# Modulation vectors of a two-block transformer: from split matmuls on TensorE to multiply-and-sum on VectorE

## The chip, the cores and the metric

One core of a Trainium2 chip runs the whole program. The metric is the time of one execution on the device in microseconds (us). The kernel before took 1823.71 us as the median of 3 runs (1823.54 to 1828.19). The profile is of one further execution, which took 1829.04 us; its span, from the first to the last instruction, is 1827.3 us. About 0.3% is what can be told from no change.

## The reference, cut to what matters

Two blocks of two layers each work on 256 tokens of width 1024. The second block also has 256 context tokens, and each of its layers is modulated by six vectors of width 1024 for the latent tokens and six for the context, made from two condition vectors `c` and `c_ctx`:

```python
def modulate(x, g, shift, scale):
    return rms_norm_2(x, g) * (1 + scale) + shift

for l in range(DEPTH):                       # 2
    need_ctx = l < DEPTH - 1
    mod_l = jnp.split((jax.nn.silu(c) @ ada_w[l] + ada_b[l])[:, None, :], 6, axis=-1)
    mod_c = jnp.split((jax.nn.silu(c_ctx) @ ada_w[l] + ada_b[l])[None, None, :], 6, axis=-1)
    hl = modulate(x_lat, norm_g[l, 0], mod_l[0], mod_l[1])
    hc = modulate(x_ctx, norm_g[l, 0], mod_c[0], mod_c[1])
    ...                                      # mixer (even_mixer, odd_mixer)
    x_lat = x_lat + mod_l[2] * (mix_l @ w_out[l])
    x_lat = x_lat + mod_l[5] * conv_ffn(modulate(x_lat, norm_g[l, 1], mod_l[3], mod_l[4]), ...)
    if need_ctx:
        ...                                  # the same for x_ctx with mod_c
```

`ada_w` is 2 x 1024 x 6144 in float32, so each layer's two products are a matrix of 1024 x 6144 times two vectors. In layer 1 the context gets only its first two vectors (shift and scale of the mixer's norm), because `need_ctx` is false there. Everything is in float32.

## The kernel before

All weights are read once, in the order of use, as units of up to 128 x 1056 float32 from one packed tensor `in_wts`. `fetch` (L471) takes the next unit: SyncE's queue starts the DMA into a slot of the ring `raw` (3 slots), ScalarE writes the rounded high half `wh` (L486), VectorE subtracts it and writes the low half `wl` (L487); these rings have 4 slots each. Every product then is three matmuls of fp32r: high by high, high by low, low by high (`tout` L506, `p_nout` L521). A low or high tile's slot comes free when the last matmul on it is done; so TensorE's progress lets ScalarE go on, and ScalarE lets VectorE go on.

The program is a list of steps (`plan` L1798), each with the units that it needs; before a step is emitted, units are fetched up to 5 ahead of it. `weave` puts two lists of steps together, evenly. The framework's scheduler then orders instructions on each engine; each engine works in that order and waits for semaphores.

The stages, with the stretch of the span that they take in the profile (read from the first and last instructions of each stage's lines, rounded): the first mixer of block 1 (0 to 200 us), FFN 0 (200 to 375), the second mixer (375 to 548), FFN 1 with the context attention of block 2 woven in (548 to 750), the even layer's mixer (750 to 1050), the third FFN, "f2" in the code (1050 to 1440), the odd layer's mixer (1440 to 1640), and the last FFN (1640 to 1827). The FFNs of block 1 work on 256 columns, the third FFN mostly on 512 (latent and context), the last on 258.

The modulation vectors are made in 24 blocks a layer, `p_ada` (L561): a block is 256 columns of `ada_w`, in two units. `csil` holds, for each 128 rows of the contraction, the two condition vectors after SiLU, split in high and low, and is the stationary operand; 16 matmuls of 256 columns accumulate four useful rows (L574 and L575). ScalarE copies them out (`adarow`, L578); two transposing products with `sel4` sum the halves and bring the result into columns (L581); VectorE adds the bias into `mods` (L583). `ADA` gives for each place of the plan how many blocks are woven in there; `ada_need(l, n)` brings the count up to what the next step needs.

Names in the rows: `acc` and `s` are PSUM tiles, `nh` and `nl` the split activations, `g`, `gh` and `gl` the gated FFN activations, `cc`, `gr`, `ur`, `ug` and `uu` FFN tiles, `o<-vx,W` and `s<-mqh,mkh` the even layer's recurrence in its parallel form.

Of the kernel before, what the change touches and what calls it, by code (L numbers as in the profile page):

```python
# [9 lines left out]
F32 = mybir.dt.float32  # L10
# [28 lines left out]
RAW_BUFS = 3  # L39
# [15 lines left out]
def unit_specs():  # L55
# [23 lines left out]
    for l in range(2):  # L79
        for i in range(24):  # L80
            halves(("ada", l, i), "ada_w_2", l, _ar(256 * i, 256))
# [94 lines left out]
def consts_all(i):  # L176
# [6 lines left out]
    cv = np.zeros((128, KD, 2), np.float32)  # L183
    cv[:, :, 0] = _tl(i["c_2"][0])
    cv[:, :, 1] = _tl(i["c_ctx_2"])
    c["cvec"] = cv.reshape(128, -1)
    s = np.zeros((128, 2))
    s[:4] = [[1, 0], [1, 0], [0, 1], [0, 1]]
    c["sel4"] = s
# [117 lines left out]
def weave(a, b, tail=0):  # L307
# [25 lines left out]
CN = 0  # L333
# [45 lines left out]
class Prog:  # L379
# [13 lines left out]
    def emit(self, tc, nc, ctx, wts, xin, cs, rpb, out, offs, probe=None):  # L393
        self.tc, self.nc, self.ctx = tc, nc, ctx
        self.wts, self.xin, self.cs, self.rpb, self.out, self.offs = wts, xin, cs, rpb, out, offs
        self.probe = probe or (lambda name, ap: None)
# [9 lines left out]

    def load_consts(self, pool, i):
# [4 lines left out]
    def start(self):  # L412
        nc = self.nc
        self.const = self.pool("const", 1)
        self.wp = self.pool("wp", 4)
        self.keep = self.pool("keep", 1)
# [29 lines left out]
        self.csil = self.keep.tile([128, 160], F32R, name="csil")  # L446
# [4 lines left out]
    def conditions(self):  # L451
        nc = self.nc
        sil = self.nat.tile([128, KD, 2], F32, name="sil")
        nc.scalar.activation(sil.rearrange("p a b -> p (a b)"), self.C["cvec"], AF.Silu)
        z = self.nat.tile([128, 128], F32, name="zz")
        nc.gpsimd.memset(z, 0.0)
        nc.scalar.activation(self.csil[:, 32:], z, AF.Copy)
        d = self.csil[:, :32].rearrange("p (k s e) -> p k s e", s=2, e=2)
        nc.scalar.activation(d[:, :, :, 0], sil, AF.Copy)
        nc.vector.tensor_sub(d[:, :, :, 1], sil, d[:, :, :, 0].bitcast(F32))  # L460
# [10 lines left out]
    def fetch(self, upto):  # L471
        nc = self.nc
        while self.next < min(upto, len(self.order)):
# [6 lines left out]
            nc.sync.dma_start(raw, src)  # L480
            h = self.wp.tile([128, nk, ncol], F32R, tag="wh", name="wh", bufs=HI_BUFS)
# [79 lines left out]
    def p_ada(self, l, i):  # L561
        steps = []
        box = Box()
        for kh in range(2):
            def f(i=i, kh=kh, box=box):
                nc = self.nc
                if kh == 0:
                    box.ps = self.acc()
                ps = box.ps
# [1290 lines left out]
```

## Time and profile before

| what | value |
|---|---|
| median of 3 runs | 1823.71 us |
| the profiled execution | 1829.04 us |
| its span | 1827.3 us |
| TensorE matmuls, weight loads busy | 1776.2 us (97%), 1686.5 us (92%) |
| VectorE busy | 1329.6 us (73%) |
| ScalarE busy | 1036.8 us (57%) |
| GpSimd busy | 66.1 us (4%) |
| TensorE clock granted, mean | 0.989 of full |
| weights and the rest from memory | 273.79 MB, 150 GB/s over the span |

Matmuls overlap: an instruction's duration in the trace is longer than the time from its start to the next one's start, and the time that it takes from TensorE is the latter. On VectorE a following instruction can start about 0.08 us before the end of the one ahead. "Idle before" and "waited for" name what ended an idle time; idle time on an engine that isn't the bound costs nothing by itself.

### The profile page before, as it was taken

The page shows a single profiled execution, that of the slowest core. Times are in us where ns is not written, and L with a number is a line of the kernel's source. Part 1 is how long each engine was busy: PE and PEld are TensorE (multiplying, and loading weights), DVE is VectorE, ACT ScalarE, POOL GpSimd, SP SyncE. Part 2 cuts the span into 40 slices and gives each one's busy share as a digit, 9 for nine tenths or more (in the row PEclk, how much of TensorE's full clock was granted, in tenths as well). Part 3 has the DMA queues.
Part 4 walks back from the last instruction along what each step waited for, and adds up shares of the span by engine and source line. Part 5 has one row for each costly group of instructions (what it writes and reads, how often), then busy time and mean ns, then how long its engine had stood idle before and what let it go on. Part 6 is the DMA issues. An engine that isn't in the chain of part 4 may idle for free.

```text
span 1827.3 us, 33701 instructions
## 1 busy us (share of the span) xinstructions
PE 1776.2 (97%) x13156; PEld 1686.5 (92%) x13156; DVE 1329.6 (73%) x2681; ACT 1036.8 (57%) x1807; POOL 66.1 (4%) x80
## 2 busy tenths in 40 slices
PE   8999999999999999999999999999999899999999
PEld 8998999999999999988988998888889899999999
DVE  6776887788878777866687796365467874669887
ACT  6776654566758667645445574243345565656554
POOL 0000000000110000000000000000000410000000
PEclk9999999999999999999999999999999999999999
DMA  7577555555554655535241463323335551245664
GB/s 242 165 224 223 175 185 175 183 184 181 154 170 156 186 169 166 177 113 173 84 137 47 139 186 127 103 93 108 101 96 153 165 161 49 85 139 171 195 188 138
DMA packets 80528, 277.03 MB, mean 152 GB/s; under 512 B 8945, under 2 KB 12145, under 8 KB 80241
## 3 DMA queue, kind: packets, MB, share of 16 engines
q1 hardware_dynamic: 79072, 272.25, 48.0%
q10 hardware_dynamic: 1296, 2.62, 0.4%
q8 instruction: 104, 1.70, 0.4%
q14 instruction: 56, 0.45, 0.1%
HBM read 273.79 MB, written 1.05 MB: 150 GB/s over the span
## 4 chain that ended last, share of the span: by engine, by line
PE 88%; DVE 6%; DMA 3%; ACT 2%; issue 1%; POOL 0%; ACTq 0%; DVEq 0%; POOLq 0%
PE acc L491 60%; PE s L491 20%; PE o L491 4%; DMA raw<-in_wts 3%; DVE wl L487 2%; ACT wh L486 2%; PE ptp L782 1%; PE tt L703 1%; PE stv L491 1%; DVE nt L1105 0%; PE ptp L772 0%; DVE nl L1108 0%; PE tt L798 0%; DVE t L734 0%; DVE x L818 0%
## 5 line engine op out<-in xcount | busy, mean ns | idle before, releaser
L486 ACT ACTIVATE wh<-raw 128x1024 fp32r<-128x1024 f32 (+2 forms) x528 | 540.6, 1031 | 474.4 <-PE acc L491 260.9
L487 DVE TENSOR_TENSOR wl<-raw,wh 128x1024 fp32r<-128x1024 f32 (+2 forms) x528 | 625.6, 1189 | 227.6 <-ACT wh L486 223.6
L491 PE MATMUL acc<-nh,wh 128*128 128x256 f32 (+2 forms) x872 | 271.5, 312 | 7.5 <-ACT wh L486 2.5
L491 PE MATMUL acc<-nh,wl 128*128 128x256 f32 (+2 forms) x872 | 270.5, 310 | 1.0 <-DVE wl L487 1.0
L491 PE MATMUL acc<-nl,wh 128*128 128x256 f32 (+2 forms) x872 | 270.2, 310 | 0.0
L491 PE MATMUL acc<-wh,nh 128*128 128x256 f32 (+2 forms) x768 | 222.5, 291 | 10.1 <-ACT nh L604 8.0
L491 PE MATMUL s<-nh,wh 128*128 128x256 f32 (+2 forms) x744 | 225.3, 303 | 0.9 <-ACT wh L486 0.9
L491 PE MATMUL s<-nh,wl 128*128 128x256 f32 (+2 forms) x744 | 225.0, 302 | 0.0
L491 PE MATMUL s<-nl,wh 128*128 128x256 f32 (+2 forms) x744 | 224.9, 302 | 0.0
L491 PE MATMUL acc<-wh,nl 128*128 128x256 f32 (+2 forms) x768 | 222.1, 291 | 0.5 <-DVE nl L1108 0.4
L491 PE MATMUL acc<-wl,nh 128*128 128x256 f32 (+2 forms) x768 | 221.3, 289 | 0.2 <-DVE wl L487 0.2
L491 PE MATMUL acc<-g,wh 128*128 128x256 f32 x1056 | 192.2, 283 | 0.5 <-DVE g L602 0.2
L491 PEld LDWEIGHTS acc<-nh,wh 128*128 128x128 f32 x872 | 166.2, 191 | 17.3 <-ACT wh L486 3.0
L491 PEld LDWEIGHTS acc<-nh,wl 128*128 128x128 f32 x872 | 166.2, 191 | 9.8 <-DVE wl L487 1.4
L491 PEld LDWEIGHTS acc<-nl,wh 128*128 128x128 f32 x872 | 166.2, 191 | 8.2
L491 PEld LDWEIGHTS acc<-g,wh 128*128 128x128 f32 x1056 | 163.2, 190 | 1.5 <-DVE x L818 0.9
L491 PEld LDWEIGHTS acc<-wh,nh 128*128 128x128 f32 x768 | 149.1, 194 | 11.3 <-ACT nh L604 8.3
L491 PEld LDWEIGHTS acc<-wh,nl 128*128 128x128 f32 x768 | 148.5, 194 | 2.3 <-DVE nl L1108 1.0
L491 PEld LDWEIGHTS acc<-wl,nh 128*128 128x128 f32 x768 | 149.0, 194 | 1.3 <-DVE wl L487 0.7
L491 PE MATMUL acc<-g,wl 128*128 128x256 f32 x528 | 147.5, 283 | 0.0
L491 PEld LDWEIGHTS s<-nh,wh 128*128 128x128 f32 x744 | 140.7, 189 | 7.1 <-ACT wh L486 1.1
L491 PEld LDWEIGHTS s<-nl,wh 128*128 128x128 f32 x744 | 140.8, 189 | 5.8
(378 smaller groups left out, 3548.3 us busy)
## 6 DMA issues: line engine op xcount, KB each, us to landing
raw<-in_wts SPq DMA_DIRECT2D x424, 512.0 KB, 4.0
raw<-in_wts SPq DMA_DIRECT2D x72, 448.0 KB, 3.3
raw<-in_wts SPq DMA_DIRECT2D x24, 384.0 KB, 3.6
x<-in_x SPq DMA_DIRECT2D x8, 256.0 KB, 6.9
raw<-in_wts SPq DMA_DIRECT2D x4, 408.0 KB, 3.0
rpb<-in_rpb ACTq DMA_DIRECT2D x1, 1536.0 KB, 8.3
raw<-in_wts SPq DMA_DIRECT2D x2, 528.0 KB, 4.0
out<-x ACTq DMA_DIRECT2D x8, 128.0 KB, 1.7
```

The lines of the kernel that those rows point to most:

```text
L486: nc.scalar.activation(hf[:, c], raw[:, c], AF.Copy)
L487: nc.vector.tensor_sub(lf[:, c], raw[:, c], hf[:, c].bitcast(F32))
L491: self.nc.tensor.matmul(o, a, b, start=start, stop=stop)
L703: self.nc.tensor.transpose(ps[:, p, t * 128:(t + 1) * 128], src[:, t, p * 128:(p + 1) * 128], self.ident)
L782: self.nc.tensor.transpose(pt[:, kb], P[:, kb * 128:(kb + 1) * 128], self.ident)
```

## The change

The host packs `ada_w` transposed, in 48 units a layer of 128 output columns by 1024 rows of the contraction, so that an output column is a partition and the sum runs along it. These units aren't split: the raw tile is used as it comes. `csil` becomes both condition vectors, broadcast to all partitions by one DMA (128 x 2048) and put through SiLU on ScalarE. For each unit VectorE multiplies the raw tile by a condition vector and sums along the partition, with the bias as start value, once for each condition, and only once (the latent condition) in layer 1 from unit 16 on. The product itself goes to a tile `junk` that nobody reads. The matmuls, the transposing products, `adarow`, `sel4` and the bias addition go.

The table `ADA` is new: 1 + 2 + 2 + 3 blocks (a block is now two units) in the first mixer, 5 in FFN 0, 7 in FFN 1, 4 in the even layer, 24 in the third FFN, none in the odd layer. In FFN 0, FFN 1 and the third FFN the units are woven over the whole stage. The raw ring has 4 slots. A pad of 64 bytes ahead of the weight pool and another behind it put the rings `raw`, `wh` and `wl` 64 bytes off a multiple of 128, and all else where it was by that measure. A DMA scratch area is made smaller, which gives the space.

```diff
-RAW_BUFS = 3
+RAW_BUFS = 4
...
-        for i in range(24):
-            halves(("ada", l, i), "ada_w_2", l, _ar(256 * i, 256))
+        for i in range(48):
+            add(("ada", l, i), "ada_w_2", l, _ar(128 * i, 128), rall)
...
+        if key[0] == "ada":
+            a = a.T
...
 ADA = {
...
-    "a1.0": 1, "o.m": 1, "a0.t": 0, "a0.1": 4, "f1": 1, "f2.0": 1, "f0": 0, "f2.1": 1, "e.3": 0, "a1.1": 2,
+    "a0.0": 1, "a0.1": 2, "a0.2": 2, "a0.3": 3, "f0": 5, "f1": 7, "e.0": 2, "e.1": 1, "e.2": 1, "f2": 24,
 }
...
+    def pad(self, name):
+        t = self.ctx.enter_context(self.tc.tile_pool(name=name, bufs=1)).tile([128, 16], F32, name=name)
+        self.nc.gpsimd.memset(t, 0.0)
...
+        self.pad("pad0")
         self.wp = self.pool("wp", 4)
+        self.pad("pad1")
...
+        c = self.csil.rearrange("p a b -> p (a b)")
+        nc.sync.dma_start(c, bass.AP(tensor=self.cond.tensor, offset=self.cond.offset, ap=[[0, 128], [1, 2 * D]]))
+        nc.scalar.activation(c, c, AF.Silu)
+        nc.gpsimd.memset(self.mods[1], 0.0)
...
             nc.sync.dma_start(raw, src)
+            if key[0] == "ada":
+                self.W[key] = raw
+                continue
...
-                h, w = self.W[("ada", l, i, kh)]
-                for k in range(4):
-                    c = 4 * (4 * kh + k)
-                    cs = self.csil[:, c:c + 128]
-                    self.mm(ps[:, :256], cs, h[:, k], kh == 0 and k == 0, False)
-                    self.mm(ps[:, :256], cs, w[:, k], False, kh == 1 and k == 3)
-                if kh == 1:
-                    row = self.small.tile([128, 256], F32, tag="adarow", name="adarow", bufs=2)
-                    nc.scalar.activation(row, ps[:, :256], AF.Copy)
-                    t = ps[:, 256:260].rearrange("p (a b) -> p a b", a=2)
-                    for c in range(2):
-                        self.mm(t[:, c], row[:, c * 128:(c + 1) * 128], self.C["sel4"], True, True)
-                    b = self.C["adab%d" % l][:, 2 * i:2 * i + 2]
-                    nc.vector.tensor_add(self.mods[l][:, 2 * i:2 * i + 2], t, b[:, :, None].to_broadcast([128, 2, 2]))
+                w = self.W[("ada", l, m)]
+                t = self.mods[l][:, m]
+                n = 1 if l == 1 and m >= 16 else 2
+                for c in range(n):
+                    nc.vector.tensor_tensor_reduce(out=self.junk, in0=w, in1=self.csil[:, c], scale=1.0,
+                                                   scalar=self.C["adab%d" % l][:, m:m + 1],
+                                                   op0=ALU.mult, op1=ALU.add, accum_out=t[:, c:c + 1])
...
-        return out + self.p_close()
+        return self.ada_need(0, 24) + weave(out, self.ada("f2")) + self.p_close()
...
-        out += self.plan_ffn1(0, self.st0, (st,), [], "an1", self.ada("f0") + (norm if CN == 0 else [])) + probe("x_f0")
+        out += self.plan_ffn1(0, self.st0, (st,), [], "an1", norm if CN == 0 else [], self.ada("f0")) + probe("x_f0")
...
-        out += self.plan_ffn1(1, self.st1, (s1, s2), [], None, self.ada("f1"), early("f1")) + probe("x_f1")
+        out += self.plan_ffn1(1, self.st1, (s1, s2), [], None, (), weave(early("f1"), self.ada("f1"))) + probe("x_f1")
```

How the order moves, on VectorE in FFN 0 first. Before, in the second third of the stage (`cc`, `gr` and `ur` are tiles of the gate, `wl` the low halves):

```order
L487 TENSOR_TENSOR wl<-raw,wh 128x1024
L602 TENSOR_TENSOR g<-cc,g 128x256
L987 SCALAR_TENSOR_TENSOR cc<-gr,c4t,cc 128x255
L990 TENSOR_TENSOR ur<-s,rrow 128x256
L987 SCALAR_TENSOR_TENSOR cc<-gr,c4t,cc 128x254
L487 TENSOR_TENSOR wl<-raw,wh 128x1024
L991 TENSOR_TENSOR cc<-cc,ur 128x256
L984 TENSOR_TENSOR gr<-acc,rrow 128x256
```

Now, in the same stage (`junk,mods_148<-raw,csil,c0t` is the product with its sum, the row with `mods_148` alone reads the sum):

```order
L976 SCALAR_TENSOR_TENSOR cc<-gr,c4t,cc 128x254
L487 TENSOR_TENSOR wl<-raw,wh 128x1024
L570 ISA junk,mods_148<-raw,csil,c0t 128x1024
L570 ISA mods_148 128x1
L591 TENSOR_TENSOR g<-cc,g 128x256
L976 SCALAR_TENSOR_TENSOR cc<-gr,c4t,cc 128x255
L980 TENSOR_TENSOR cc<-cc,ur 128x256
L979 TENSOR_TENSOR ur<-s,rrow 128x256
L487 TENSOR_TENSOR wl<-raw,wh 128x1024
L570 ISA junk,mods_148<-raw,csil,c0t 128x1024
```

The products stand one at a time between the steps of the gate.

The second place is TensorE in the even layer's recurrence, at the scores `s<-mqh,mkh` of a head. Before:

```order
L491 MATMUL acc<-wl,csil 128x256
L491 MATMUL acc<-wh,csil 128x256
L491 MATMUL s<-mqh,mkh 128x512
L491 MATMUL s<-mql,mkh 128x512
L491 MATMUL acc<-wh,csil 128x256
L491 MATMUL s<-mqh,mkl 128x512
L491 MATMUL acc<-wl,csil 128x256
```

Now:

```order
L491 MATMUL acc<-nh_134,wl 128x512
L491 MATMUL acc<-nh_135,wh 128x512
L491 MATMUL acc<-nl_143,wh 128x512
L491 MATMUL s<-mqh,mkh 128x512
L491 MATMUL s<-mql,mkh 128x512
L491 MATMUL o<-vx,W 128x129 x7
L491 MATMUL s<-mqh,mkl 128x512
L491 MATMUL acc<-nh_135,wl 128x512
```

The scores were surrounded by modulation matmuls (`csil`) and now stand among projections (`nh`, `nl`).

## Rows read from the trace of the kernel before

**Rows 1.** Part 1 of the page: busy us, share, instructions

```profile
PE 1776.2 (97%) x13156; PEld 1686.5 (92%) x13156; DVE 1329.6 (73%) x2681; ACT 1036.8 (57%) x1807; POOL 66.1 (4%) x80
```

**Rows 2.** Part 4 of the page: the chain that ended last, by engine

```profile
PE 88%; DVE 6%; DMA 3%; ACT 2%; issue 1%; POOL 0%; ACTq 0%; DVEq 0%; POOLq 0%
```

**Rows 3.** Windows by stage: stretch, length, busy us of each engine (instructions), clock, DMA

```profile
core 0: us, PE busy (x) PEld busy (x) DVE busy (x) ACT busy (x) POOL busy (x), PEclk, DMA share, GB/s
0.00:200.00 200.00, 187.80 (x1518) 183.90 (x1518) 143.20 (x289) 136.37 (x260) 3.88 (x17) 1.00 0.66 210
200.00:375.00 175.00, 173.29 (x1442) 173.23 (x1442) 138.18 (x240) 97.94 (x150) 0.87 (x1) 0.99 0.58 180
375.00:548.00 173.00, 170.99 (x1431) 170.29 (x1430) 141.18 (x332) 110.83 (x234) 12.70 (x14) 0.99 0.56 173
548.00:750.00 202.00, 198.37 (x1667) 197.47 (x1667) 158.59 (x316) 147.75 (x241) 0.60 (x3) 1.00 0.54 170
750.00:1050.00 300.00, 284.41 (x1953) 261.46 (x1953) 218.60 (x544) 152.99 (x311) 12.92 (x15) 0.96 0.39 122
1050.00:1440.00 390.00, 385.86 (x2110) 334.09 (x2110) 248.19 (x377) 175.57 (x252) 8.27 (x9) 1.00 0.41 127
1440.00:1640.00 200.00, 194.32 (x1540) 186.27 (x1540) 124.00 (x240) 112.16 (x211) 25.25 (x20) 0.98 0.35 106
1640.00:1827.00 187.00, 181.18 (x1508) 179.75 (x1507) 157.65 (x348) 103.20 (x153) 1.62 (x1) 1.00 0.56 172
```

**Rows 4.** Waits: who waited for whom, us in total, times, longest

```profile
ACT wh L486 <- PE acc L491: 260.9, 175, 5.7
ACT wh L486 <- DMA raw<-in_wts: 102.5, 91, 3.4
```

**Rows 5.** Timeline of TensorE in a modulation block: start us, us, instruction

```profile
55.76 0.28 PE L491 MATMUL acc<-wl,csil 128*128 128x256 f32 x1
...
58.60 0.28 PE L491 MATMUL acc<-wl,csil 128*128 128x256 f32 x1
```

**Rows 6.** Timeline of TensorE at the four small matmuls of a block

```profile
60.33 0.50 PE L491 MATMUL acc<-c0t,adarow 128*128 128x2 f32 x4
60.69 0.37 PE L491 MATMUL acc<-wl,nh 128*128 128x264 f32 x1
```

**Rows 7.** Windows by stage, instructions on csil alone: their sum

```profile
sum 1827.00, PE 110.06 PEld 97.69 DVE 0.17 ACT 0.51; mean PE 13.76 PEld 12.21 DVE 0.02 ACT 0.06
```

**Rows 8.** Groups by form on VectorE: count, busy us, mean ns, idle before

```profile
L487 DVE TENSOR_TENSOR wl<-raw,wh 128x1024 fp32r<-128x1024 f32 x424 | 517.5, 1224 | 196.1 <-ACT wh L486 193.1 <-PE acc L491 0.8 <-PE ht L1482 0.6
L602 DVE TENSOR_TENSOR g<-cc,g 128x256 fp32r<-128x256 f32 x44 | 18.3, 419 | 3.0 <-ACT g L601 2.6
L583 DVE TENSOR_TENSOR mods<-acc,c0t 128x4 f32<-128x4 f32 x48 | 7.3, 154 | 7.7 <-PE acc L491 7.6
```

**Rows 9.** Timeline of VectorE in FFN 1, back to back

```profile
698.98 1.22 DVE L487 TENSOR_TENSOR wl<-raw,wh 128x1024 fp32r<-128x1024 f32 x1 [0.55 <-ACT wh L486]
700.13 0.42 DVE L602 TENSOR_TENSOR g<-cc,g 128x256 fp32r<-128x256 f32 x1
```

**Rows 10.** Timeline of VectorE in the odd mixer: reductions over 256 columns

```profile
1551.09 0.48 DVE L1764 CUSTOM_DVE_ANT_0 s<-s,rpb,nm 128x256 f32<-128x256 f32 x1
1551.49 0.49 DVE L1764 CUSTOM_DVE_ANT_0 s<-s,rpb,nm 128x256 f32<-128x256 f32 x1
```

**Rows 11.** Timeline of TensorE in the even layer: a wait for VectorE

```profile
963.19 1.26 PE L1482 MATMUL ht<-c0t,hs 128*128 128x128 f32 x4 [2.20 <-DVE hs L1481]
```

**Rows 12.** Window of the even layer just behind (columns as in rows 3)

```profile
963.60:970.50 6.90, 6.12 (x15) 4.50 (x15) 5.96 (x17) 1.57 (x4) 0.75 (x1) 0.51 0.00 0
```

**Rows 13.** Groups by form on TensorE: the last FFN (258) and others (256)

```profile
L491 PE MATMUL s<-nh,wh 128*128 128x258 f32 x176 | 49.6, 282 | 0.0
L491 PE MATMUL s<-nh,wh 128*128 128x256 f32 x432 | 122.3, 284 | 0.9 <-ACT wh L486 0.9
```

More of the change, by code (lines that the diff above doesn't have):

```diff
@@ L182, in consts_all @@
     c["an0"] = _tl(i["attn_norm"][0])
[L183 to L189, printed above, removed]
     return c
@@ L391, in __init__, with emit @@
         self.utab = unit_table(self.order, self.specs)
-    def emit(self, tc, nc, ctx, wts, xin, cs, rpb, out, offs, probe=None):
+    def emit(self, tc, nc, ctx, wts, xin, cs, rpb, cond, out, offs, probe=None):
         self.tc, self.nc, self.ctx = tc, nc, ctx
         self.wts, self.xin, self.cs, self.rpb, self.out, self.offs = wts, xin, cs, rpb, out, offs
+        self.cond = cond
         self.probe = probe or (lambda name, ap: None)
@@ L445, in start @@
             nc.gpsimd.memset(self.half[64 * e:64 * e + 64, 2 + e:3 + e], -0.125)
-        self.csil = self.keep.tile([128, 160], F32R, name="csil")
+        self.csil = self.keep.tile([128, 2, D], F32, name="csil")
+        self.junk = self.keep.tile([128, D], F32, name="junk")
         self.nh = [self.keep.tile([128, NT], F32R, name="nh%d" % k) for k in range(KD)]
@@ L562, in p_ada, with f @@
         steps = []
-        box = Box()
-        for kh in range(2):
-            def f(i=i, kh=kh, box=box):
+        for m in (2 * i, 2 * i + 1):
+            def f(m=m):
                 nc = self.nc
-                if kh == 0:
-                    box.ps = self.acc()
-                ps = box.ps
-                h, w = self.W[("ada", l, i, kh)]
-                for k in range(4):
-                    c = 4 * (4 * kh + k)
-                    cs = self.csil[:, c:c + 128]
-                    self.mm(ps[:, :256], cs, h[:, k], kh == 0 and k == 0, False)
-                    self.mm(ps[:, :256], cs, w[:, k], False, kh == 1 and k == 3)
-                if kh == 1:
-                    row = self.small.tile([128, 256], F32, tag="adarow", name="adarow", bufs=2)
-                    nc.scalar.activation(row, ps[:, :256], AF.Copy)
-                    t = ps[:, 256:260].rearrange("p (a b) -> p a b", a=2)
-                    for c in range(2):
-                        self.mm(t[:, c], row[:, c * 128:(c + 1) * 128], self.C["sel4"], True, True)
-                    b = self.C["adab%d" % l][:, 2 * i:2 * i + 2]
-                    nc.vector.tensor_add(self.mods[l][:, 2 * i:2 * i + 2], t, b[:, :, None].to_broadcast([128, 2, 2]))
-            steps.append(((("ada", l, i, kh),), f))
+                w = self.W[("ada", l, m)]
[5 more added lines that the diff above has]
+                                                   op0=ALU.mult, op1=ALU.add, accum_out=t[:, c:c + 1])
+            steps.append(((("ada", l, m),), f))
         return steps
@@ L1610, in plan_ffn2a @@
                     out += steps(x, j, key + (x, j), slice(0, NT))
-            out += self.ada("f2.%d" % t) + self.ada_need(0, 24)
-            if t == 2:
-                out += self.ada_need(1, 8)
             if t < 2:
@@ L1833, in host_arrays @@
         "in_rpb": rpb_layout(inputs),
+        "in_cond": np.concatenate([np.asarray(inputs["c_2"]).reshape(-1), np.asarray(inputs["c_ctx_2"]).reshape(-1)]),
     }
@@ L1843, in build @@
     cs = [a["in_c%d" % j] for j in range(len(offs))]
-    prog.emit(tc, nc, ctx, a["in_wts"], a["in_x"], cs, a["in_rpb"], out, offs, probe)
+    prog.emit(tc, nc, ctx, a["in_wts"], a["in_x"], cs, a["in_rpb"], a["in_cond"], out, offs, probe)
 def kernel(**inputs):
@@ L1853 @@
     arrays, offs = host_arrays(prog, inputs)
-    nc = _bacc.Bacc("TRN2", target_bir_lowering=False, num_devices=1)
+    nc = _bacc.Bacc("TRN2", target_bir_lowering=False, num_devices=1, dynamic_dma_scratch_size=1024)
     with _tile.TileContext(nc, schedule_with_timeline_sim=True) as tc, ExitStack() as ctx:
```

8 lines of the change are left out of this document (removed), and 2 rows, old and new, of the table ADA.

## The prediction

> **What bounds the kernel now.** I read the busy times first, then the chain that ended last, then the busy time of each engine in eight windows, one per stage, then single lines. TensorE is busy 1776.2 us of the span of 1827.3 us, 97% [rows 1], and it holds 88% of the chain that ended last [rows 2]. Between the eight windows this differs: in the two middle FFN windows (200 to 375 and 548 to 750 us) TensorE is busy 173.29 of 175 us and 198.37 of 202 us, and in the window of the even layer (750 to 1050 us) 284.41 of 300 us at a granted clock of 0.96 [rows 3]. VectorE has 138 to 159 us in the two FFN windows, 79%, and at most 84%, in the last window [rows 3]. ScalarE waits 260.9 us in all for TensorE to give back a high-weight buffer, and only 102.5 us for a weight DMA [rows 4]: TensorE sets the pace and the others are held back by it.
>
> **What is taken from TensorE.** The modulation vectors are 48 blocks of 256 columns, each two weight units, 16 matmuls of 256 columns, and two transposing products of fp32, which the trace records as four matmuls with 2 columns. In a stretch without a break, 24 steps from 55.76 to 58.60 us take 2.84 us, 0.118 us a matmul [rows 5]; 16 make 1.89 us. A group of four small ones starts at 60.33 us and the next matmul at 60.69 us, 0.36 us [rows 6]. Coming in and out of such a group costs about two further starts of 0.2 us where 0.12 is usual, so I take 2.5 us a block and 120 us for all. The busy time of the 768 is 110.06 us [rows 7], which counts overlapping ends too, so 110 to 125 us bounds it.
>
> Blocks before, by stage (from the table ADA and the `ada_need` calls): 16 in the first mixer, 6 in the second, 1 in FFN 1, 16 in the even layer, 2 in the third FFN, 7 in the odd mixer. At 2.5 us the full relief is 40, 15, 2.5, 40, 5 and 17.5 us.
>
> **What VectorE gets.** Gone: 96 low-half subtractions of 1224 ns [rows 8]; back to back one starts 1.15 us after the other (698.98 to 700.13 us) [rows 9], 110 us; and 48 small additions of 154 ns [rows 8], 7 us. New: 160 products with a sum over 1024 columns (96 for layer 0; 32 + 32 for layer 1, where the context condition is left out from m = 16), each with a small instruction that reads the sum. The trace has none of this size. The nearest is the 256-column form with a pointer as start value: two stand 0.40 us apart with their reads [rows 10]. Going from 256 to 1024 columns takes a plain two-input operation from 419 to 1224 ns [rows 8], 1.05 ns a column, hence 0.40 + 0.81 = 1.21; I take 1.25 us. Ends: 1.15 us (a subtraction alone) and 1.44 us (all durations with no overlap). So 200 us come, 117 go, +83 us on VectorE.
>
> By stage the blocks are now 8, FFN 0 5, FFN 1 7, even 4, third FFN 24, odd none, 5.0 us of VectorE each in layer 0. VectorE's load becomes: first mixer 143 + 1 us; FFN 0 138 + 25 = 163 of 175 us (93%); FFN 1 159 + 33 = 191 of 199 us (96%; at 1.44 us a product 98%); third FFN 248 + 75 = 323 of 385 us (84%); even 219 - 19; odd 124 - 17. In FFN 0 the products stand between the evacuations and the subtractions, not in a block. The wait added is for the weight DMA at the head of VectorE; behind it stand a subtraction, for which TensorE waits, and the evacuations that free its PSUM tiles. TensorE has up to four split units in hand, 2.8 us each (24 matmuls of 0.118 us), so a delay of a few us is hidden by these, and without the cover it would be lost one for one.
>
> **What of the relief arrives.** The first mixer has 40 us less of matmul, but its 144 us of VectorE in the 160 left are 90%, above all that this trace shows; at the 84% of the last window it would take 171 us, so I count 28. In the other mixers VectorE stays under 84%, but the removed matmuls filled the waits of softmax and recurrence, so I let part arrive: seven tenths in the even layer (28 of 40), where TensorE already waits 16 of 300 us, and a little more where it waits less, 12 of 15 in the second mixer and 13 of 17.5 in the odd one; third FFN 2 of 5. FFN 0 and FFN 1 lose nothing if VectorE can be filled to 96%; at 90% FFN 0 would take 163/0.9 = 181 us (+6) and FFN 1 212 us (+10); I take +3 for each. The condition load is 1 MB at the front of the weight queue; at the 210 GB/s of the first window [rows 3] it takes 5 us, of which the 34% free DMA time hides part: +3 (0 to 5). Clock: after a wait of 2.20 us for VectorE [rows 11] the clock granted is 0.51 from 963.6 to 970.5 us [rows 12], its lower level of 1.2 GHz, which costs half of the 6.9 us, 3.4; with fewer filler matmuls I add one: +3. Sum: -28 - 12 - 28 - 13 - 2 + 3 + 3 + 3 + 3 = -71 us.
>
> In the even layer weight loads are busy 261.46 of 300 us, 87%, while matmuls are busy 95% [rows 3]; read by the loads, 39 us of this window are room that the removed matmuls may only have filled. I read it by the matmuls, since the third FFN also has loads busy 334 of 390 us, 86%, with matmuls at 99%: 512-column matmuls leave the loads idle. The other reading is a rival below. The Trainium skill (Perfetto Trace Analysis, Identifying the Most-Contended Engine) is on its side: it holds that matmul busy time misjudges how full TensorE is, and that the busy time of weight loads judges it better.
>
> **The weight rings 64 bytes off.** No row shows weights at such a place. Nearest: in the last FFN the moving operand starts 8 bytes short of a multiple of 128, and its 258-column matmuls take 282 ns, against 284 ns for 256 columns from an even place [rows 13]. So 0 to 2 ns less on at most 12,196 matmuls (13,156 [rows 1] less the 960 removed), 0 to -24 us. A loss isn't excluded: by the half ns to which these means are rounded, +6. I take -4, near nothing, because the ends of matmuls are modelled and the difference may be the model's. The fourth raw slot I cost at nothing: it covers the modulation unit that now keeps a slot until VectorE is done; without it the 102.5 us of DMA waits [rows 4] would grow.
>
> Total -75. The profiled execution took 1829.04 us, its span 1827.3; that makes 1754, and as the median of the runs, 1823.71, is 0.3% lower, 1748 us.
>
> **Rivals.**
> *TensorE was the only bound* (0.22). For it: TensorE is busy 171 of 173 us in the second mixer [rows 3], and the others wait through back-pressure [rows 4]. Against it: VectorE at 90% and more. Whole relief of 120, rings -4, start +3: 1829 - 121, as a median about 1703 (1685 to 1725).
> *VectorE becomes the bound* (0.14) at the 84% that the last window shows: FFN 0 163/0.84 = 194 (+19), FFN 1 191/0.84 = 228 (+26), first mixer 144/0.84 = 171 (-29), third FFN -5, the rest as above -53, start +3: -39, median about 1785. Against it: the products are spread, and nothing says that 84% is the most.
> *The removed matmuls filled room* (0.06): by the 87% of the loads the even layer gives none of its 28 us: -71 + 28 - 4 = -47, median 1777. For it: 16 idle us of TensorE there in spite of the filler. Against it: weight loads are busy 93% in the odd mixer and 98% in the second, where little room can be.
> *Slower: the product with sum takes two cycles a column* (0.05). Its form with two inputs from SBUF isn't in the trace; the known one reads PSUM. Against it: the plain subtraction has two inputs from SBUF and takes 1.05 ns a column. Then a pair takes 2.3 us: FFN 0 138 + 46 = 184, at 90% 204 us (+29); FFN 1 156 + 64 = 220, 245 us (+43); third FFN 243 + 147 = 390, 433 us (+43); first mixer 103 + 74 = 177, 197 us (-3); the rest -53, start and clock +6: +65, median 1889. It decides from about 1.8 us a pair.
> *No gain* (0.05): the softmax and scan chains of all mixers keep their length and only the holes show. Then the rest of the sum stands alone, -2 + 3 + 3 + 3 + 3 - 4 = +6: median 1830. For it: VectorE and ScalarE run at 51 to 82% in the mixers [rows 3], so chains of them may be late next. Against it: TensorE holds 88% of the chain.
>
> **How the numbers follow.** Forecast 0.48, 1748 us, own range 1725 to 1772. The range of 8 in 10 takes most of the first two rivals: 1690 to 1795. A change under 0.3% (5.5 us) can't be told from none here. Faster 0.90 (the forecast and the first three rivals), same 0.03 and slower 0.07 (the slow product, and no gain split between both).
>
> **What would show it.** Products of 1.2 to 1.4 us with reads that add under 0.1; TensorE's busy time down by 110 to 125; FFN 0 and FFN 1 as long as before within 3 us with VectorE at 90% and more; the mixers 10 to 30 us shorter each; 256-column matmuls still near 0.12 us apart. Wrong would be: TensorE waiting for the low halves in the FFN windows, matmul starts clearly closer or wider apart (then the rings do it), or a mixer as long as before.

## The result, and the profile after

The changed kernel takes 1767.66 us as the median of 4 runs (1765.52 to 1772.43), the kernel before on the same chip 1824.24 us: a ratio of 0.9689, 95% interval 0.9665 to 0.9713, or 56.6 us less. 1748 us was forecast with an own range of 1725 to 1772 and an outer one of 1690 to 1795. The profiled execution took 1765.52 us, 63.5 us less than the 1829.04 us of the one before. The sum further down explains these 63.5 us, since the forecast's -75 was made against the same execution.

Busy time of each engine, as in [rows 1]:

```profile
PE 1671.9 (95%) x12196; PEld 1570.6 (89%) x12196; DVE 1388.5 (79%) x2856; ACT 930.8 (53%) x1663; POOL 61.2 (3%) x82
```

The chain that ended last, as in [rows 2]:

```profile
PE 70%; DVE 15%; DMA 6%; issue 4%; ACT 4%; POOL 0%; SPq 0%; DVEq 0%; ACTq 0%; POOLq 0%
```

TensorE held 88% of the chain and now holds 70%; VectorE and the weight transfers hold 21% where they held 9%. Windows by stage, columns and stages as in [rows 3] (length; busy us of TensorE, its weight loads, VectorE, ScalarE, GpSimd, each with its instructions; clock; DMA):

```profile
0.00:169.00 169.00, 152.24 (x1198) 147.09 (x1198) 143.93 (x310) 102.11 (x208) 3.94 (x19) 0.97 0.63 211
169.00:341.00 172.00, 169.90 (x1465) 169.38 (x1464) 155.74 (x278) 100.55 (x155) 0.69 (x1) 0.99 0.67 215
341.00:499.00 158.00, 152.66 (x1280) 150.61 (x1279) 128.53 (x317) 95.56 (x215) 11.77 (x14) 0.98 0.47 148
499.00:707.00 208.00, 197.43 (x1659) 193.97 (x1659) 179.00 (x358) 143.77 (x233) 0.60 (x3) 0.99 0.61 193
707.00:978.00 271.00, 242.85 (x1614) 219.70 (x1613) 207.90 (x548) 117.88 (x268) 13.97 (x15) 0.94 0.30 96
978.00:1360.00 382.00, 368.89 (x1955) 313.75 (x1953) 288.43 (x445) 158.35 (x224) 1.39 (x2) 0.99 0.54 172
1360.00:1576.00 216.00, 204.14 (x1492) 193.54 (x1493) 126.22 (x253) 107.76 (x211) 27.26 (x27) 0.91 0.27 86
1576.00:1763.70 187.70, 183.74 (x1547) 182.54 (x1545) 158.75 (x353) 104.78 (x154) 1.62 (x1) 1.00 0.53 171
```

TensorE idles 92 us in all where it idled 51. The granted clock is down in the first mixer (0.97), the even layer (0.94) and the odd mixer (0.91). Waits, as in [rows 4]:

```profile
ACT wh L486 <- PE acc L491: 256.4, 155, 7.0
...
DVE junk L570 <- DMA raw<-in_wts: 72.3, 50, 4.0
ACT wh L486 <- DMA raw<-in_wts: 65.9, 42, 3.8
```

Groups by form on VectorE, answering to [rows 8]: 96 low halves of 1024 columns fewer, 160 products more.

```profile
L487 DVE TENSOR_TENSOR wl<-raw,wh 128x1024 fp32r<-128x1024 f32 x328 | 400.2, 1223 | 68.2 <-ACT wh L486 67.2
L570 DVE CUSTOM_DVE_ANT_0 junk<-raw,csil,c0t 128x1024 f32<-128x1024 f32 x160 | 204.9, 1281 | 72.5 <-DMA raw<-in_wts 72.3
```

To see where the time went I compare marks: the end of ScalarE's activation of one and the same weight unit in each trace, one unit near each stage's end. ScalarE runs up to four units ahead of TensorE, so a mark can move by some us from one stage to the next where other units stand between. The stages, in us:

| stage | before | after | difference | forecast |
|---|---|---|---|---|
| first mixer | 196.6 | 164.7 | -32.0 | -28, load +3 |
| FFN 0 | 175.1 | 170.3 | -4.8 | +3 |
| second mixer | 139.1 | 127.3 | -11.8 | -12 |
| FFN 1 | 228.7 | 234.8 | +6.1 | +3 |
| even layer | 311.9 | 285.2 | -26.7 | -28 |
| third FFN | 357.5 | 368.7 | +11.2 | -2 |
| odd mixer | 191.6 | 185.4 | -6.2 | -13 |
| last FFN | 217.0 | 215.4 | -1.6 | 0 |
| not placed | | | | rings -4, clock +3 |

The relief of the second mixer and the even layer is as forecast, that of the first mixer larger; the odd one got half of it. The third FFN, which was to gain 2 us by the forecast, pays 11.

Two places show how. First VectorE at the head of the third FFN, start and length of each instruction:

```profile
1033.44 1.28 DVE L570 CUSTOM_DVE_ANT_0 junk<-raw,csil,c0t 128x1024 f32<-128x1024 f32 x1
1034.65 0.08 DVE L570 DVE_READ_ACCUMULATOR2_ANT mods<- 128x1 f32 x1
1034.65 1.22 DVE L487 TENSOR_TENSOR wl<-raw,wh 128x1024 fp32r<-128x1024 f32 x1
1035.78 0.48 DVE L1561 SCALAR_TENSOR_TENSOR ug<-acc,c3t,ug 128x255 f32<-128x255 f32 x1
1036.18 0.47 DVE L1562 SCALAR_TENSOR_TENSOR uu<-s,c3t,uu 128x255 f32<-128x255 f32 x1
1036.57 0.41 DVE L591 TENSOR_TENSOR gl<-uu,gh 128x256 fp32r<-128x256 f32 x1
1036.90 1.28 DVE L570 CUSTOM_DVE_ANT_0 junk<-raw,csil,c0t 128x1024 f32<-128x1024 f32 x1
```

No idle time stands between them: a product takes 1.21 us of VectorE with its read (1033.44 to 1034.65), and the low half and the evacuations that TensorE waits for queue behind it. Here the stage works on 256 columns at a time, not yet on 512. From 978 to 1080 us TensorE waits most for the two halves of the weights, and from 978 to 1060 us ScalarE, which makes the high half, waits for raw data (2.5 us at the same place before):

```profile
PE acc L491 <- ACT wh L486: 5.1, 4, 1.8
PE acc L491 <- DVE wl L487: 4.5, 3, 2.5
...
ACT wh L486 <- DMA raw<-in_wts: 23.8, 14, 3.8
```

In the kernel before, VectorE had little room in this head already, 52 of 56 us:

```profile
1051.00:1107.00 56.00, 54.13 (x423) 52.22 (x422) 52.01 (x96) 40.76 (x69) 0.00 (x0) 1.00 0.61 180
```

Second, the odd mixer: three stretches of equal length, columns as above.

```profile
1462.10:1492.80 30.70, 28.78 (x232) 27.20 (x231) 12.71 (x31) 14.23 (x35) 1.64 (x1) 1.00 0.18 53
1492.80:1523.50 30.70, 29.92 (x131) 27.18 (x131) 9.53 (x27) 11.49 (x26) 0.00 (x0) 0.50 0.00 1
1523.50:1554.20 30.70, 30.18 (x236) 27.77 (x236) 18.05 (x39) 15.94 (x28) 0.00 (x0) 1.00 0.31 104
```

In the middle one the granted clock is 0.50, the level of 1.2 GHz, and TensorE does 131 matmuls where its neighbours do 232 and 236, although it is busy all the time. At its start TensorE waits 1.78 us for a softmax (from 1491.8 us). The clock records show 102.4 us at this level in the whole span, before 41.0; between the marks of the odd mixer it is 37.5 us, before 10.2.

### The profile page after: what moved, and what is told of

Its sections match the earlier page's. It is cut to its first block, busy times and chain, and to the rows that moved or that the text cites. A ratio compares the mean times of both kernels' runs of the same rounds, so it can differ in the third digit from the quotient of the medians.

```text
span 1763.7 us, 31647 instructions
## 1 busy us (share of the span) xinstructions
PE 1671.9 (95%) x12196; PEld 1570.6 (89%) x12196; DVE 1388.5 (79%) x2856; ACT 930.8 (53%) x1663; POOL 61.2 (3%) x82
## 4 chain that ended last, share of the span: by engine, by line
PE 70%; DVE 15%; DMA 6%; issue 4%; ACT 4%; POOL 0%; SPq 0%; DVEq 0%; ACTq 0%; POOLq 0%
PE acc L491 47%; PE s L491 16%; DMA raw<-in_wts 6%; DVE wl L487 5%; PE o L491 4%; DVE junk L570 3%; ACT wh L486 1%; PE ptp L771 1%; PE tt L692 1%; PE stv L491 0%; POOL rs L612 0%; ACT L978 0%; DVE t L723 0%; DVE x L807 0%; DVE nt L1094 0%
## 5 line engine op out<-in xcount | busy, mean ns | idle before, releaser
L486 ACT ACTIVATE wh<-raw 128x1024 fp32r<-128x1024 f32 (+4 forms) x432 | 439.4, 1024 | 399.6 <-PE acc L491 256.4
L487 DVE TENSOR_TENSOR wl<-raw,wh 128x1024 fp32r<-128x1024 f32 (+4 forms) x432 | 508.3, 1181 | 80.0 <-ACT wh L486 78.4
L570 DVE CUSTOM_DVE_ANT_0 junk<-raw,csil,c0t 128x1024 f32<-128x1024 f32 x160 | 204.9, 1281 | 72.5 <-DMA raw<-in_wts 72.3
L491 PE MATMUL acc<-g,wh 128*128 128x256 f32 x1056 | 188.3, 280 | 3.7 <-ACT g L590 1.5
L491 PEld LDWEIGHTS acc<-wh,nh 128*128 128x128 f32 x768 | 147.0, 192 | 10.9 <-ACT nh L593 7.4
```

Source lines behind the costliest of these rows:

```text
L486: nc.scalar.activation(hf[:, c], raw[:, c], AF.Copy)
L487: nc.vector.tensor_sub(lf[:, c], raw[:, c], hf[:, c].bitcast(F32))
L491: self.nc.tensor.matmul(o, a, b, start=start, stop=stop)
L570: nc.vector.tensor_tensor_reduce(out=self.junk, in0=w, in1=self.csil[:, c], scale=1.0, scalar=self.C["adab%d" % l][:, m:m + 1], op0=ALU.mu ...
```

## The experiments

Each time is a median, each ratio against the kernel before on the same chip, which took 1822.7 to 1824.24 us on the chips used. Stage figures are differences between the marks above, in one profiled execution of each run.

**The rings.** Theory A: the 64 bytes shorten matmuls by as much as the starts show. Theory B: about 4 us, as forecast. The pads were taken out of the changed kernel, put alone into the kernel before, and made 128 bytes.

```diff
-        self.pad("pad0")
         self.wp = self.pool("wp", 4)
-        self.pad("pad1")
```

> The changed kernel with the two 64-byte pads taken out, so that the weight rings start at the same place in a partition's 128 bytes as before; everything else of the change stays. Theory A (rings are worth what the traces show: in the changed kernel 256-column matmuls of a stretch start 115.9 ns apart on average, in the kernel before 119.1, and there are 8008 of them, while 512-column ones are 1.4 ns further apart, 1584 of them): about 3.2 x 8008 = 26 us are due to the rings, of which some lies in stretches where TensorE waits: time 1782 to 1792 us, 256-column starts back at 119 ns, 512-column ones at 231.8, and the last FFN, whose work the change does not touch, longer by 3 to 4 us. Theory B (the forecast's term of -4): 1769 to 1774 us, starts still 116 ns apart because the removed products made the difference.

Measured: 1777.96 us, 10.3 more than with the pads; ratio 0.9747 (0.9727 to 0.9767). FFN 0 is 6.0 us longer, the even layer 3.8, the others under 2, the last FFN 1.0 where 3 to 4 were expected. 256-column matmuls start 119.1 ns apart again. TensorE at the same 25 matmuls of FFN 0 with the pads, first and last:

```profile
180.00 0.28 PE L491 MATMUL s<-nl,wh 128*128 128x256 f32 x1
...
182.72 0.28 PE L491 MATMUL acc<-nl,wh 128*128 128x256 f32 x1
```

And 25 without them:

```profile
180.05 0.28 PE L489 MATMUL s<-nh,wh 128*128 128x256 f32 x1
...
182.91 0.28 PE L489 MATMUL acc<-nh,wh 128*128 128x256 f32 x1
```

24 steps take 2.72 and 2.86 us, 0.113 and 0.119 us each, while the shown duration is 0.28 us in both.

```diff
+        self.pad("pad0")
         self.wp = self.pool("wp", 4)
+        self.pad("pad1")
```

> The kernel before with the two 64-byte pads alone; modulation vectors stay on TensorE. Theory A (rings): 256-column starts near 116 ns, 3.2 ns less on 8776 matmuls is 28 us, 512-column ones 1.4 ns more on 1584, +2: 1796 to 1803 us. Theory B (-4): 1816 to 1824 us.

Measured: 1810.00 us, 12.9 less than before, ratio 0.9921 (0.9905 to 0.9937); FFN 0 8.2 us shorter. 256-column matmuls start 116.0 ns apart on average in place of 119.1, 512-column ones 233.1 in place of 231.8.

```diff
-    ...tile([128, 16], F32, name=name)
+    ...tile([128, 32], F32, name=name)
```

> The changed kernel with pads of 128 bytes in place of 64, so that the rings move by a whole 128 bytes. Theory A (the 64 bytes off a multiple of 128 are what shortens the 256-column matmuls): starts back at 119 ns, 512-column ones at 231 to 232, time as with the pads taken out, 1774 to 1781 us. Theory B (any other place of the rings does it, or the pads' own tiles): 116 ns, 1764 to 1770 us.

Measured: 1775.29 us, ratio 0.9732 (0.9719 to 0.9745), starts back at 119.1 and 231.4 ns. So the place modulo 128 bytes does it, not the pads. Theory B falls, and A too in its size: the starts speak for 26 us, and 8 to 13 arrive, 6 to 8 of them in FFN 0. The 8 of e9 are too few by what the clock gave it, since it has 82.8 us at half speed against 102.4 in the changed kernel. Why FFN 1, where TensorE was nearly as busy as in FFN 0 (98% and 99% [rows 3]), gained only 1.9 us in e2 is open.

**The fourth raw slot.**

```diff
-RAW_BUFS = 4
+RAW_BUFS = 3
```

> The changed kernel with 3 raw slots in place of 4. Theory A (the slot is needed, because a modulation unit keeps its slot until VectorE has done both products): ScalarE's and VectorE's waits for raw data grow (65.9 and 72.3 us now), FFN 0, FFN 1 and the head of the third FFN get longer: 1780 to 1810 us. Theory B (slots are no limit, the DMA rate or VectorE is): 1764 to 1770 us.

Measured: 1805.64 us, 38 more, ratio 0.9910 (0.9887 to 0.9934): theory A, beyond the middle of its range. The third FFN loses 22 us, the first mixer 7, FFN 0 5.5; the last FFN's 7 are a shift of the marks, since the odd mixer ahead of it is 3 us and the stretch behind the last mark 4 us shorter. ScalarE's and VectorE's waits for raw data:

```profile
ACT wh L486 <- DMA raw<-in_wts: 167.2, 129, 4.6
DVE junk L570 <- DMA raw<-in_wts: 89.9, 50, 4.9
```

**VectorE's price.** Products cut to 64 columns; all else stands. The sums leave out 960 columns, so only the time counts.

```diff
-out=self.junk, in0=w, in1=self.csil[:, c], ...
+out=self.junk[:, :64], in0=w[:, :64], in1=self.csil[:, c, :64], ...
```

> The changed kernel with each of the 160 products taken over 64 of the 1024 columns; the other 960 columns of the modulation vectors are left out. Weight transfers, raw slots, order and the reads of the sums stay, only VectorE's time goes: a product takes about 0.2 us in place of 1.28, 160 x 1.08 = 173 us of VectorE less. Theory A (VectorE's load sets what of the relief arrives: +12 us in the third FFN, +7 in FFN 1 and a part of the mixers): 1735 to 1748 us, with the head of the third FFN at a TensorE share of 93% or more and FFN 1 as long as before. Theory B (the products' wait for their transfers at the head of VectorE is what costs, whatever they take themselves): 1758 to 1768 us. Theory C (clock and the mixers' own chains): the same, 1760 to 1768, but with the waits for raw data gone.

Measured: 1718.92 us, ratio 0.9426 (0.9410 to 0.9441), 48.7 less than the changed kernel, more than any theory gave. By stage: FFN 1 -17.6, third FFN -10.7, first mixer -8.6, FFN 0 -5.6, the mixers behind it -2.1 at most each. A product now takes 281 ns, and VectorE is busy 1242.9 us in place of 1388.5. Its windows of FFN 0 and FFN 1:

```profile
160.00:325.00 165.00, 165.00 (x1446) 165.00 (x1446) 137.42 (x270) 96.53 (x147) 1.61 (x1) 1.00 0.66 215
...
480.00:675.00 195.00, 193.75 (x1673) 192.67 (x1672) 158.79 (x360) 146.74 (x236) 0.00 (x0) 1.00 0.64 204
```

VectorE's waits for the product's transfer grew, to 86.9 us, while the time fell. Theory B (the wait is the price) falls, A is confirmed in kind and was too small: 146 us of VectorE cost 49 us, with all that followed from them. The lower clock is part of that: the time at half speed fell from 102.4 to 68.3 us, which is worth up to 17 of the 49 us. In FFN 1, which pays most, the starts of TensorE's matmuls stand over 0.3 us later than their size asks 6 times before (6.7 us in all), 18 times after (17.8 us) and 3 times here (4.7 us). The largest wait that the changed kernel's trace names there is for the softmax of the context attention, which is woven into this stage:

```profile
PE ptp L771 <- ACT sm L1324: 4.8, 6, 1.9
```

**The head of the third FFN.**

```diff
-        return self.ada_need(0, 24) + weave(out, self.ada("f2")) + self.p_close()
+        h = len(out) // 4
+        return self.ada_need(0, 24) + out[:h] + weave(out[h:], self.ada("f2")) + self.p_close()
```

> The changed kernel with the 24 blocks of modulation products of the third FFN woven into the last three quarters of its steps, none in the first quarter. Theory A (the third FFN loses its 10 us in its first 80 us, where VectorE is busy 77 of 80 us with the evacuations and the products come on top; later TensorE is full anyway): the third FFN shorter by 8 to 11 us, TensorE's busy share in its first 80 us from 86% back to 93% or more, total 1755 to 1760 us. Theory B (products wait for their DMA at the head of VectorE wherever they stand): the loss moves to the later part, total 1763 to 1770 us.

Measured: 1760.26 us, ratio 0.9655 (0.9637 to 0.9672), 7.4 less than the changed kernel. The head and the rest of the stage, between the same two weight units, in the changed kernel:

```profile
982.00:1057.00 75.00, 63.65 (x445) 58.72 (x444) 74.34 (x134) 43.14 (x73) 0.00 (x0) 0.95 0.62 197
1057.00:1348.00 291.00, 289.96 (x1382) 240.22 (x1381) 200.37 (x284) 105.43 (x138) 0.30 (x1) 1.00 0.51 162
```

And with the products late:

```profile
975.00:1033.00 58.00, 55.70 (x432) 53.20 (x431) 55.97 (x102) 40.14 (x69) 1.54 (x1) 0.97 0.60 190
1033.00:1344.00 311.00, 301.64 (x1416) 249.35 (x1415) 231.47 (x338) 105.73 (x141) 1.41 (x1) 0.98 0.53 171
```

The head is 17 us shorter, 58 us, about what it took before: VectorE was busy 74.34 of 75 us there and held TensorE. The rest is 20 us longer, so theory A is right on the head and wrong on the stage: between its marks the third FFN takes 372.7 us, 4.0 more than in the changed kernel, where 8 to 11 less were expected. The loss moved to the later part, as theory B has it. What the total gained came in the even layer (-6.5) and the odd mixer (-8.5), which has 23.9 us at half speed here against 37.5. One of the places where the late products cost, VectorE, ScalarE and TensorE in order of start:

```profile
1189.56 1.28 DVE L570 CUSTOM_DVE_ANT_0 junk<-raw,csil,c0t 128x1024 f32<-128x1024 f32 x1 [3.03 <-DMA raw<-in_wts]
...
1191.77 0.74 DVE L1561 SCALAR_TENSOR_TENSOR uu<-s,c3t,uu 128x510 f32<-128x510 f32 x1
...
1194.06 0.63 ACT L590 ACTIVATE gh<-uu 128x512 fp32r<-128x512 f32 x1 [5.30 <-DVE uu L1574]
1194.74 0.50 PE L491 MATMUL acc<-gh,wh 128*128 128x512 f32 x1 [3.76 <-ACT gh L590]
```

The product waits 3.03 us for its transfer at the head of VectorE, behind it the evacuation `uu`, behind that `gh`, and TensorE waits 3.76 us; 3.4 us at a clock of 0.50 follow at 1195.3 us. TensorE waits twice for `gh` in this part, 9.2 us in all.

**The clock in the odd mixer.**

```diff
+DUMMY = {"o.1": 3, "o.2": 2, "o.3": 1, "o.m": 1}
+            ps = self.acc()
+            for q in range(16):
+                self.mm(ps[:, :256], self.nh[q % 8][:, :128], self.nl[q % 8][:, :256], q == 0, q == 15)
```

> The changed kernel with 7 blocks of 16 filler matmuls of 256 columns on operands that lie in SBUF anyway, put at the places of the odd mixer where the kernel before had its 7 modulation blocks; their results are not used. Theory A (clock: TensorE's gap of 1.78 us at 1491.8 us falls into a stretch with few matmuls, and the 30.7 us at a granted clock of 0.50 behind it cost 15 us): the stretch is gone or at most 7 us long, the filler costs 112 x 0.117 = 13 us at most, less in gaps; 1752 to 1765 us. Theory B (the stretch comes in any case): 1770 to 1780 us.

Measured: 1762.80 us, ratio 0.9664 (0.9641 to 0.9687). The odd mixer is 6.4 us shorter between its marks with 112 matmuls more. The stretch, around the same place:

```profile
1470.00:1500.00 30.00, 30.00 (x247) 28.98 (x245) 12.66 (x24) 13.26 (x35) 1.64 (x1) 1.00 0.14 42
1500.00:1530.00 30.00, 29.48 (x241) 27.86 (x240) 12.87 (x43) 14.25 (x30) 1.64 (x1) 1.00 0.09 26
```

The long stretch is gone, as theory A has it, and the mean clock of all four runs is 0.980 to 0.982, where the changed kernel's four have 0.969 to 0.972. That the wait of 1.78 us brought the stretch isn't shown. In e4 a stretch of 13.7 us begins at 1485.5 us, ahead of the same wait (1487.1 us); e10, below, has a wait of 1.67 us in this mixer and no long stretch; e11 has 27.3 us behind a wait of 0.75 us. That the whole kernel is faster by it is not shown either, since the two intervals overlap.

**Was the even layer's relief real work?**

```diff
+DUMMY = {"e.a": 2, "e.0": 4, "e.2": 1, "e.d": 1, "e.e": 4}
```

> The changed kernel with 12 such filler blocks in the even layer, at places where the kernel before had modulation blocks. Theory A (the removed blocks of the even layer only filled TensorE's waits there, 28 of 271 us idle now, and the clock: five half-speed stretches of together 37 us from 840 to 1008 us against three of 17 us): the filler costs nothing or wins, 1755 to 1768 us. Theory B (the relief of the even layer, 27 us, was real work on the path): 12 x 16 x 0.117 = 22 us come back, 1780 to 1792 us.

Measured: 1787.03 us, ratio 0.9803 (0.9786 to 0.9819): 19.4 more, of 22 that 192 matmuls of 0.117 us make. Theory B. Between the marks the even layer is 12.4 us longer, the third FFN 10.6, and FFN 1 2.3 shorter; the last 64 filler matmuls run just ahead of the even layer's end mark (973.4 to 985.7 us, mark at 992.8), so a part of their cost can show behind it. The filler didn't help the clock there either: the half-speed time in the span is 102.4 us with it and without it.

**Where the products stand.**

```diff
-"f2": 24,
+"f2": 8, "o.0": 2, "o.1": 4, "o.2": 4,
```

> The changed kernel with 16 of the 24 modulation blocks of layer 1 moved from the third FFN into the odd mixer, where VectorE is busy 126 of 216 us; 8 stay, spread over the third FFN. Theory A (VectorE's load where TensorE has no room sets the loss): the third FFN gets back 6 to 10 us of its 10, the odd mixer gets to 167 of 216 us of VectorE and loses at most 3: 1757 to 1763 us. Theory B (a product costs TensorE about the same wherever it stands): 1763 to 1770 us. Theory C (in the odd mixer the products delay the softmax chain, whose waits let the clock fall): 1772 to 1785 us.

Measured: 1747.50 us, ratio 0.9587 (0.9569 to 0.9606), 20.2 less than the changed kernel and faster than any of the three theories. The third FFN is back at 358.5 us. The odd mixer and the last FFN together are 6.5 us shorter in spite of the products, with 10.2 us at half speed against 40.9: no theory had that. Here the last of the 8 blocks stood behind the normalisation that reads them, so part of what it reads was unset, and only the time counts. In the next version they stand ahead of it:

```diff
+        h, q = len(out) // 4, len(out) - 20
+        return self.ada_need(0, 24) + out[:h] + weave(out[h:q], self.ada("f2")) + out[q:] + self.p_close()
```

> The changed kernel with 8 blocks of layer 1 woven into the third FFN between its first quarter and its last 20 steps, so that they stand ahead of the normalisation that reads them, and the other 16 in the odd mixer. Theory A (a product costs where VectorE has no room: in the third FFN's first 80 us none is left, in the odd mixer 42%): third FFN 358 to 362 us between its marks as against 368.7, the odd mixer without a long half-speed stretch, 1745 to 1754 us. Theory B (a product costs TensorE alike in all stages, 49 us for 160 as the run with short products gave): 1764 to 1770 us.

Measured: 1743.37 us, ratio 0.9558 (0.9542 to 0.9574), 24.3 less than the changed kernel and a little under theory A's range: the shortest of the runs that do the whole work. The third FFN takes 353.2 us between its marks, 15.5 less. Third FFN and odd mixer:

```profile
970.00:1330.00 360.00, 357.30 (x1902) 304.42 (x1901) 257.25 (x392) 152.31 (x217) 2.24 (x2) 1.00 0.43 137
1330.00:1552.00 222.00, 204.28 (x1572) 193.48 (x1572) 170.50 (x331) 113.59 (x221) 39.68 (x27) 0.95 0.51 166
```

TensorE is busy 99% of the third FFN again, and the odd mixer takes 3.8 us more between its marks with VectorE at 77%, without a long half-speed stretch. The products aren't free there: the odd mixer and the last FFN together are 2.2 us shorter than in the changed kernel, but 20.4 us fewer at half speed should give about 10. That filler or products keep the long stretch away is likely but not sure, as the next run shows.

```diff
-"f0": 5, "f1": 7,
+"f0": 5, "a1.0": 1, "a1.1": 1, "a1.2": 1, "a1.3": 1, "f1": 3,
```

> As e10, and 4 of the 7 blocks of FFN 1 moved to the second mixer, one to each of its four heads' steps. Short products made FFN 1 17.6 us shorter for 7 blocks, 2.5 us a block. Theory A (the load of VectorE in FFN 1, 86%, decides, and the second mixer with 81% has room): FFN 1 8 to 10 us shorter, the second mixer 0 to 3 us longer, 1737 to 1746 us. Theory B (the second mixer has no room either, its relief of 10 us goes): FFN 1 shorter by as much as the second mixer is longer, 1745 to 1754 us.

Measured: 1760.38 us, ratio 0.9629 (0.9602 to 0.9657), outside both theories. FFN 1 is 12.9 us shorter than in e10, the second mixer 18.5 longer, and the odd mixer, planned as in e10, 10.9 longer. In the second mixer TensorE waits for a softmax step, for which it did not wait in the changed kernel, and VectorE has a product ahead of such a step:

```profile
PE s L491 <- DVE nm L743: 5.8, 5, 2.1
...
446.03 1.27 DVE L570 CUSTOM_DVE_ANT_0 junk<-raw,csil,c0t 128x1024 f32<-128x1024 f32 x1
447.23 0.08 DVE L570 DVE_READ_ACCUMULATOR2_ANT mods<- 128x1 f32 x1
447.23 0.28 DVE L743 CUSTOM_DVE_ANT_0 sm<-s,c4t 128x128 f32<-128x128 f32 x1
```

`sm` and `nm` (L743) are one step, its tile and its reduction. The waits of 5.8 us explain a part of the 18.5; 13.7 us at half speed, where e10 has none in this mixer, are worth up to 7 more, and the rest is open. The profiled execution has a stretch of 27.3 us at 0.50 in the odd mixer, which e10 has not. The six runs fall in two groups: four of 1760.20 to 1761.58 us with mean clocks of 0.967 to 0.972, two of 1745.35 and 1750.28 us with 0.979 and 0.975. The latter lie in theory B's range; what the long stretch adds, neither theory had.

```diff
-"f1": 7, "e.0": 2, "e.1": 1, "e.2": 1,
+"f1": 4, "e.0": 3, "e.1": 2, "e.2": 2,
```

> As e10, and 3 of the 7 blocks of FFN 1 moved to the even layer's steps. Short products made FFN 1 shorter by 2.5 us a block and the even layer by 1.9 us for its 4 blocks. Theory A (the price is set by the stage): FFN 1 7 to 8 us shorter, the even layer 1 to 3 us longer, 1736 to 1741 us. Theory B (as in the second mixer of e11, where 4 blocks cost 18 us, products between the steps of a softmax or recurrence hold its chain up): the even layer 10 us longer or more, 1745 to 1755 us.

Measured: 1745.35 us, ratio 0.9569 (0.9549 to 0.9589), no different from e10. FFN 1 gains 7.3 us as theory A has it, the even layer loses 11.1 as B has it. There TensorE waits longer for the recurrence's `hs`, and 6.8 us more at half speed are worth up to 3.4 us:

```profile
PE ht L1472 <- DVE hs L1471: 16.8, 4, 4.5
```

In e10 these were 3 waits and 12.6 us:

```profile
PE ht L1471 <- DVE hs L1470: 12.6, 3, 4.5
```

These waits are 4.2 of the 11.1 us.

## Why the prediction was right, and where its sizes were off

**Bound and relief.** The forecast stands within its own range, and TensorE was the bound, and taking the blocks away was worth real time: right. The busy time fell by 104.3 us, under the 110 to 125 forecast, but two other things are in it. The rings shorten it by about 20.5 (e2: 1752.7 us against 1776.2 [rows 1], less 3.0 for 5.9 us fewer at half speed), and 61.4 us more at half speed lengthen it by about 30.7. That leaves, as an estimate, 104.3 - 20.5 + 30.7 = 114.5 us for the 48 blocks, 2.4 us each, where 2.5 was taken. The rival that the removed matmuls only filled room fell with e7. The Trainium skill (Perfetto Trace Analysis, Identifying the Most-Contended Engine), which calls matmul busy time a poor measure of how full TensorE is and goes by its weight loads (and its share of peak arithmetic), was on that rival's side. Here that reading misled: in the even layer the loads are busy 219.70 of 271 us after, and the filler still cost 19 of 22 us.

**The product.** 1.21 us with its read against 1.25 taken: right, and the two-cycle rival fell. VectorE's busy time rose by 58.9 us where +83 was counted; the products account for 6 of the difference (160 x 0.04), and of the rest it is only known that instructions which follow back to back overlap by 0.08 us, and a fuller VectorE has more of them.

**FFN 0 and FFN 1.** VectorE runs at 91% of FFN 0 with TensorE busy 169.90 of 172 us, without harm beyond the 5.6 us that e5 gave back; so the rival that 84% is a limit fell. Without the rings FFN 0 costs +1.2 (e1), with them -4.8. FFN 1 cost +6.1 for +3, and its term was mis-sized by more than that: at 86% VectorE's time for the products costs 17.6 us there (e5), the most of all stages. The forecast took the load of the stage; the waits for the softmax woven into it (4.8 us after, none of them in e5) were not in it, and they are only a part. Why the stage is 11.5 us shorter than before in e5, with one block of 2.5 us gone, is open.

**The mixers.** First, second and even came within 7 us of the part of the relief that was counted. In the even layer the holes do show: starts of TensorE that stand over 1 us later than the matmul ahead asks make 29.2 us there after, 13.8 before.

**The third FFN.** This is the step that failed: "third FFN 248 + 75 = 323 of 385 us (84%)", hence 2 of 5 us of relief, where 11.2 us were lost. The mean load was even lower than counted, 76% (288.43 of 382 us), so the mean of the stage does not set the price. At the head, where the products stand between 256-column evacuations, VectorE had little room before and is full after (74.34 of 75 us), and the head takes 75 us in place of 56; further on TensorE is fully busy again. The head isn't the only place that can pay: with no products there (e4) all of them cost as much in the later part. That VectorE's time for the products is the cause is shown by e5 (10.7 us back) and by e8 and e10, with 16 blocks fewer in the stage (10.2 and 15.5 back). Mis-sized by 13 us.

**The odd mixer and the clock.** -13 was counted and -6.2 came; "With fewer filler matmuls I add one: +3" became 61.4 us more at the lower level, some 31 us lost over the kernel, which the stage differences above contain. In the odd mixer it is 27.3 us more, about 14 us lost: without them it would have gained some 20 us, so the relief was there and the clock took it. The largest stretch alone, 30.7 us, costs about 13 (131 matmuls for 234), and with filler it is gone (e6).

**The rings.** -4 was counted and 8 to 13 came. The prediction compared shown durations (282 and 284 ns [rows 13]), which the ring's place does not change: the gain is in the distance of the starts alone, 119 to 116 ns, which the prediction had named as a sign of being wrong. Beyond the 4 counted they gave 4 to 9 us: by luck they paid for a third to two thirds of the third FFN's 13, and without them the time would stand at 1775.29 (e9) or 1777.96 us (e1), outside the forecast's own range.

**The raw slot.** Costed at nothing with its cover named; e3 puts a price on the cover, 38 us.

In sum, stage by stage against the forecast: worse by 13.2 us in the third FFN, 6.8 in the odd mixer, 3.1 in FFN 1 and 1.3 in the even layer; better by 7.8 in FFN 0 (6.0 of it the rings), 7.0 in the first mixer (its load of the conditions, counted at 3, can't be seen in it) and 1.6 in the last FFN. With the 1 us of rings and clock that was not placed this is 9 us, and 2 more lie behind the last mark: -63.5 in place of -75. The rival "TensorE only bound" (1703 us) is what is left if VectorE's time is nearly taken out: 1718.92 in e5; the other 16 us are not explained.

## What to carry to other kernels

Work moved to an engine with a mean load of 76% in a stage still costs where that engine is full for 75 us; read the load in short windows at the heads of stages before weaving evenly, and put the work where the engine has room and nothing in a chain stands behind it (the odd mixer here, not the second mixer). Read a matmul's cost from start to start, since durations hide a change of 3%. When filler is taken from a latency-bound stage, count the time at the lower clock in that stage, and look at several executions (the even layer's filler gave none of it back, the odd mixer's most).

## What the runs showed of the hardware

A place of the weights 64 bytes off a multiple of 128 shortens 256-column fp32r matmuls from 119.1 to 116.0 ns from start to start and lengthens 512-column ones from 231.8 to 233.1 ns (e2); 128 bytes off changes nothing (e9). In the changed kernel the starts are 115.4 ns apart where the weights are the stationary operand (`acc<-g,wh`, 119.3 before) and 117.1 where they are the moving one (`acc<-wh,nh`, 119.2 before); the rows name the moving operand first.

A half-speed stretch can last 30.7 us while TensorE is busy 97% of it. In all seven profiled executions whose odd mixer is that of the changed kernel (it, e1, e3, e4, e5, e7, e9) the longest one there has 13.7 to 30.7 us; with filler (e6) none has over 3.4, with products e8 and e10 have none over 6.8, e12 10.2 and e11 27.3 us. What starts and what ends it is open. A product over 64 columns takes 281 ns where one over 1024 takes 1281, so about 1.04 ns a column and 0.21 us beside.
